# A streaming-encoder block on one core: a head's exponentials, normalisation, turning and values products on later steps, and the gates' functions 16 steps behind GpSimd's additions

## The chip, the core and the metric

The kernel runs on one core of a Trainium2 chip. The time is device time in microseconds (us). The engines are called as the profile calls them: PE is TensorE (its weight loads are PEld), DVE is VectorE, ACT is ScalarE, POOL is GpSimd, SP is SyncE, which here only issues DMAs.

## The reference

One layer over L = 512 tokens of width D = 2048, in float32. `proj = rmsnorm(x) @ w_in` is cut into the parts of two mixers and two merge gates. What the change touches, from the reference:

```python
logits = jnp.einsum('bqhd,bqkhd->bqkh', q_c, k_sel) * scale + bias      # 8 heads, head dim 128
logits = jnp.where(sel_ok[..., None], logits, -jnp.inf)                 # chunk-causal top-k keys
probs = jax.nn.softmax(logits, axis=2)
a_out = einsum('bqkh,bqkhd->bqhd', probs, v_sel) * jax.nn.silu(az)
b_out = retention_mixer(rq, rk, rv, ret_gn_gain) * jax.nn.silu(rz)
merged = jax.nn.sigmoid(ga) * (a_out @ w_a_out) + jax.nn.sigmoid(gb) * (b_out @ w_b_out)
r = x + merged @ w_o
return r + (p_i @ w_ple) * jax.nn.sigmoid(r @ w_ple_gate)               # and a last rmsnorm
```

The selection is kept as a mask over all keys, so that a head is a dense, causal attention over 512 tokens with a mask that is added to its bias.

## The kernel before

**Pairs.** A projection by two blocks of 128 weight columns (a pair) is done as seven Strassen-like products of 16 matmuls each (`gemm_pair`). Float32 is emulated with high and low parts: of each product's weights (128x1024) ScalarE casts the high part `wh` (L139) and VectorE subtracts it to get the low part `wl` (L144). Eight matmuls of 512 columns use `wh`, eight of 256 use `wl`; products 1, 4 and 6, counted from 0, begin with `wl`, the others with `wh`. Products 0 to 6 go to the PSUM banks `ps_v`, `ps_p`, `ps_q`, `ps_r`, `ps_p`, `ps_v`, `ps_p`. Behind a product ScalarE copies a bank (`pv` after product 0, `e` of L240 after products 1, 4 and 6), and VectorE subtracts or adds that copy to another bank (`e_t`, L244) after products 2, 5 and, twice, 6. Product 6 adds into the bank that `e` copies after product 4, so it starts behind that copy. A second function joins two `e_t` to the result; for a gate pair it adds on GpSimd (L960) where `adder=pool`, for a head's queries and keys on VectorE (L1041, `aq` and `ak`).

**Steps.** The program is issued in one order. Every two matmuls of a pair are one step, so that a product is 8 steps and a pair 56 (`PAIR_STEPS`); `later(n, f)` issues `f` n steps further on, and what is due at one step is issued in the order in which it was asked for. This decides where an instruction stands in the queue of its engine, and no engine passes over an instruction that waits. The weights' splits are issued two products ahead, at a product's first step, `wl` one step behind `wh`; there are three buffers each for `wh` and `wl`, and a split uses the one that the product before has given back. The raw weights are loaded by SP (7 buffers); some products need a second block added, by an accumulating DMA that GpSimd issues (L104) or by VectorE (L146).

**Order of the stages that the change touches.** Four pairs of `rz` (about 780 to 891 us): `b_out` (L1007) has ScalarE's Silu on the result `go`, GpSimd's multiplication with the retention output, and a DMA to `bd`, also issued by GpSimd. VectorE still does part of the top-k there (L723 to L726). Three pairs of `az` (891 to 951): Silu on ScalarE (L969) and a DMA to `zd` from ScalarE (L970). In both, `gate_pair` (L952) has `later(1, finish)` on L963: the function is issued one step behind GpSimd's second addition of that half. A pair's first half gets its second addition at step 48, the second half at 56.

Then eight pairs `u_qk`, one for each head (951 to 1145). A head's attention (`attention_head`, L1018) is issued during the next pair: four logits products (L1056, L808 to L810) with VectorE's addition and row maximum (L1058), the negated maximum `nm` (L1063) and four exponentials with their sums on ScalarE (`exps`, L1066), the reciprocal `ri` (L1070), the multiplication by it (`normalize`, three on ScalarE at L1076, one on VectorE at L1074), ten transpositions on TensorE (`turn`, L1085, `ps_pt`), their high parts `pth` on ScalarE (`high`, L1091 and L1094), the low parts `ptl` on VectorE (`low`, L1099), the values products (`outs`, L1111 and L1113, `ps_o`) already in the pair after that, the copy `oT` (L1117) and its store to `od`. The numbers in `steps` (L1122 to L1129) are the steps from the start of the pair that follows the head's own. Every three values products need a `ptl`: the first `outs` uses the one of 384 columns, the second the one of 256, the third the one of 512.

Last the fourth `az` pair (about 1145 to 1171), with the steps of head 7 and the loads and splits of `b_out` (`b_load`, `bk`, `bh`, `bl`), and the product with `w_b` (`project_b`), during which `a_load` fetches the heads' outputs and `zd`, multiplies them on GpSimd (L1152) and splits them for the product with `w_a`.

Of the kernel before, what the change touches and what calls it, by code (L numbers as in the profile page):

```python
# [34 lines left out]
def block_kernel(tc, xT, pT, posb, posq, w_in, w_v, w_k, w_a, w_b, w_o, w_ple, w_gate,  # L35
                 w_gt, w_pt, fgb, tab, xg, cst, dec, out, out_a, out_b):
    nc = tc.nc
    pe, dve, act, pool, sp = nc.tensor, nc.vector, nc.scalar, nc.gpsimd, nc.sync

    with contextlib.ExitStack() as ctx:  # L40
# [10 lines left out]
        def U(name, dt=F32):  # L51
            return up.tile([128, L], dt, name=name, tag="u")

        def B(name, dt=F32):
            return bp.tile([128, 1280], dt, name=name, tag="b")

        def P(name):
            return pp.tile([128, L], F32, name=name, tag="p")
# [4 lines left out]
        def tok(t):  # L63
            return slice(128 * t, 128 * t + 128)
# [96 lines left out]
        def later(n, f):  # L161
            if n <= 0:
                return f()
            tick[1] += 1
            heapq.heappush(soon, (tick[0] + n, tick[1], f))
# [49 lines left out]
        def alt(t, q):  # L215
            return t.rearrange("p (a s c) -> p a s c", s=2, c=64)[:, :, 0 if q == LO else 1, :]

        def fit(t, like):
            return t.rearrange("p (a c) -> p a c", c=like.shape[2]) if len(like.shape) == 3 else t
# [175 lines left out]
        for k in range(KT):  # L395
# [7 lines left out]
            elif k < 10:  # L403
                t = U("xk")
                sp.dma_start(t, xT[:, k, :])
                xs.append(t)
            elif k % 2 == 0:
                t = B("xk2")
# [390 lines left out]
        def split(src, name, lag=0):  # L799

            h = U(name + "h", F32R)
            l = U(name + "l", F32R)
            later(lag, lambda: act.activation(h, src, AF.Copy))
            later(lag and lag + 1, lambda: dve.tensor_sub(l, src, h.bitcast(F32)))
            return h, l
# [7 lines left out]
        yd, bd, od, zd = (dp.tile([NH, 128, L], F32, name=n) for n in ("yd", "bd", "od", "zd"))  # L813
# [138 lines left out]
        def gate_pair(ids, finish, wide=256, adder=None):  # L952
            t = B("go")
            outs = [t[:, 0:512], t[:, 512:1024]]
            have = [0, 0]

            def done(c0, c1, i, q):
                o = outs[i]
                to = alt(o, q)[:, 4 - wide // 64:, :]
                (adder or dve).tensor_add(to, fit(c0, to), fit(c1, to))  # L960
                have[i] += 1
                if have[i] == 2:
                    later(1, lambda: finish(i, o))  # L963

            gemm_pair(ids, Xh, done, wide=wide)

        def to(dst, func):
            def finish(i, o):
                act.activation(o, o, func)  # L969
                act.dma_start(dst[i], o)  # L970
            return finish
# [45 lines left out]
        aparts = []  # L1017
        def attention_head(h):  # L1018
            E = {}
# [30 lines left out]
            def logits(t):  # L1050
                ln = 128 * (t + 1)
                ps = P("ps_l")
                if t:
                    three(ps[:, :ln], E["aqs"], E["aks"], tok(t), slice(0, ln))
                else:
                    pe.matmul(ps[:, :ln], E["aq"][:, tok(t)], E["ak"][:, 0:ln], start=True, stop=True)  # L1056
                lg = E["bm"][:, TOFF[t]:TOFF[t] + ln]
                dve.tensor_tensor_reduce(out=lg, in0=ps[:, :ln], in1=lg, scale=1.0, scalar=-3e38,  # L1058
                                         op0=OP.add, op1=OP.max, accum_out=mx[:, t:t + 1])
# [20 lines left out]
            def turn(i):  # L1080
                ps = E["pt", i] = P("ps_pt")
                js = [(0, t) for t in range(4)] if i == 0 else [(1, 1), (1, 2), (1, 3), (3, 3)] if i == 1 \
                    else [(2, 2), (2, 3)]
                for n, (j, t) in enumerate(js):
                    pe.transpose(ps[:, tok(n)], E["bm"][:, TOFF[t] + 128 * j:TOFF[t] + 128 * j + 128], ident)  # L1085

            def high(i):
                if i == 0:
                    E["p"] = B("pth", F32R), B("ptl", F32R)
                n = (512, 384, 256)[i]  # L1090
                act.activation(E["p"][0][:, JOFF[i]:JOFF[i] + n], E["pt", i][:, 0:n], AF.Copy)  # L1091
                if i == 1:
                    E["p3"] = U("p3")
                    act.activation(E["p3"][:, 0:128], E["pt", i][:, 384:512], AF.Copy)  # L1094

            def low(i):
                n = (512, 384, 256)[i]
                c = slice(JOFF[i], JOFF[i] + n)
                dve.tensor_sub(E["p"][1][:, c], E["pt", i][:, 0:n], E["p"][0][:, c].bitcast(F32))  # L1099
# [4 lines left out]
            def outs(n):  # L1104
                if n == 0:
                    E["po"] = P("ps_o")
                po = E["po"]
                for i in range(3 * n, min(3 * n + 3, len(seq))):
                    a, b, j = seq[i]
                    if j == NT - 1:  # L1110
                        pe.matmul(po[:, 384:], E["v"][0][:, tok(3)].bitcast(F32), E["p3"][:, 0:128], start=False, stop=False)  # L1111
                    else:
                        pe.matmul(po[:, 128 * j:], E["v"][a][:, tok(j)], E["p"][b][:, JOFF[j]:JOFF[j] + L - 128 * j],  # L1113
                                  start=(i == 0), stop=(i == len(seq) - 1))
                if n == 3:
                    E["oT"] = U("oT")
                    act.activation(E["oT"], po, AF.Copy)  # L1117

            def store():
                sp.dma_start(od[h], E["oT"])  # L1120

            steps = [(-30, loads), (-8, mask), (30, values_load)]  # L1122
            steps += [(n, lambda t=t: logits(t)) for t, n in enumerate((20, 22, 24, 26))]
            steps += [(28, exps), (34, normalize)]
            steps += [(50, lambda i=i: turn(i)) for i in range(3)]
            steps += [(n, lambda i=i: high(i)) for i, n in enumerate((52, 52, 54))]
            steps += [(n, lambda i=i: low(i)) for i, n in enumerate((54, 54, 56))]
            steps += [(n, lambda i=i: outs(i)) for i, n in enumerate((65, 65, 69, 69))]
            steps += [(73 + STORE_LAG // 2, store)]  # L1129
            return done, steps  # L1130

        for n in range(Z_FIRST):
# [2 lines left out]
        for h in range(NH):  # L1135
            done, steps = attention_head(h)
            for n, f in steps:
                later(PAIR_STEPS + n, f)
            gemm_pair(u_qk[h], Xh, done)

        bparts = []

        def b_load(h):
            t = U("bk")
            sp.dma_start(t, bd[h])
            later(25, lambda: bparts.append(split(t, "b", 1)))

        def a_load(h):
            t, z = U("ak"), U("z")
            sp.dma_start(t, od[h])  # L1150
            sp.dma_start(z, zd[h])
            later(25, lambda: pool.tensor_mul(z, z, t))  # L1152
            later(29, lambda: aparts.append(split(z, "a", 1)))

        for n in range(Z_FIRST, NH // 2):
            if n == NH // 2 - 1:
                for h in range(NH):
                    later(4 + 3 * h, lambda h=h: b_load(h))
            gate_pair(u_az[n], to(zd[2 * n:2 * n + 2], AF.Silu), adder=pool)

        gates = collections.deque()
# [15 lines left out]
        for h in range(NH):  # L1177
            later(30 + 8 * h, lambda h=h: a_load(h))
# [6 lines left out]
        for m in PAIRED:  # L1185
            t = B("sm")
            s, o = t[:, 0:512], t[:, 512:1024]
# [96 lines left out]
        for m in range(MF):  # L1284
            i = u_p[m // 4][0]
# [3 lines left out]
            h, l = loaded[i]  # L1289
            ps = P("ps_pw")  # L1290
            for k in range(2):
                a, b = pparts[k]
# [5 lines left out]
            if m < Y_APART or m >= Y_APART + 2:  # L1298
                t = U("pw")
            else:  # L1300
                if m == Y_APART:
                    ypair[m // 2] = B("y2")
                t = ypair[m // 2][:, L * (m % 2):L * (m % 2) + L]
# [44 lines left out]
        for n in range(MF // 2):  # L1348
            t = B("go")
            outs = t[:, 0:512], t[:, 512:1024]  # L1350
# [108 lines left out]
        for o, c in zip(pw, HALF):  # L1459
            for j, (i, k) in enumerate(seq):  # L1460
                h, l = loaded[i]
                a, b = pparts[j][0][:, C3], pparts[j][1][:, C3]
# [23 lines left out]
        o = [U("yo") for _ in range(3)] + [s]  # L1486
# [32 lines left out]
Z_FIRST = 3  # L1519
ROUND_GAP = 11  # L1520
STORE_LAG = 16
# [97 lines left out]
```

## Time and profile before

| what | value |
|---|---|
| median of 3 timed runs | 1697.66 us (1697.63 to 1697.82) |
| profiled execution | 1698.91 us, of which the span shown is 1697.0 us |
| mean granted TensorE clock | 0.992 |
| busy PE, DVE, ACT, POOL | 98%, 81%, 55%, 18% of the span |
| instructions | 26283 |
| waits of PE between 780 and 1170 us | 27.0 us in 19 waits |
| waits of PE elsewhere | 1.8 us in the list of the largest |

All windows and times in the trace are us from the start of the span. In a row of the timeline stand the start, the duration, engine, line, operation, output and inputs with their shapes, and how many alike are joined ("x8"); a bracket gives how long the engine had been idle and what ended that. Matmuls overlap, so the distance between starts is what a group costs. In a row of the windows stand the busy times of PE, its weight loads, DVE, ACT and POOL, each with the number of instructions, then the granted clock, the DMA share and GB/s.

### The profile page before, as it was taken

The numbers are of one execution on the slowest core, as the hardware profiler recorded it, in microseconds if no ns is written. First come the engines' busy times: TensorE is split into PE (matmuls) and PEld (weight loads), VectorE is DVE, ScalarE is ACT, GpSimd is POOL, SyncE is SP. The second block draws the span as 40 slices with busy tenths as digits, with TensorE's granted clock in tenths as the row PEclk, the third lists the DMA queues.
The fourth block names the chain that finished last, engine by engine and source line by source line (L and its number), as shares of the span: only waits on it lengthen the run. The fifth ranks groups of instructions, "written<-read, shape, count | busy, mean of one in ns | idle before, by whom it ended". The sixth has DMA issues, their size and how long they took to land.

```text
span 1697.0 us, 26283 instructions
## 1 busy us (share of the span) xinstructions
PE 1660.6 (98%) x9600; PEld 1464.9 (86%) x9600; DVE 1369.1 (81%) x2189; ACT 939.4 (55%) x1437; POOL 305.3 (18%) x311
## 2 busy tenths in 40 slices
PE   9999999999999999999899999999999999999998
PEld 7999998888888888888778888888888888888897
DVE  8789887888889889889887676766548888899895
ACT  6557665555555555555444655565224455477673
POOL 3011111111111111112443111111200033411211
PEclk9999999999999999999999999999999999999999
DMA  8779888787887888877778987868866599999873
GB/s 292 263 236 254 210 206 203 198 215 184 224 215 202 212 212 212 212 209 219 215 187 217 246 193 213 213 177 272 285 237 196 159 253 284 265 323 238 217 241 125
DMA packets 141281, 379.02 MB, mean 223 GB/s; under 512 B 15328, under 2 KB 29792, under 8 KB 141152
## 3 DMA queue, kind: packets, MB, share of 16 engines
q1 hardware_dynamic: 105376, 261.20, 44.2%
q0 software_dynamic: 28144, 103.30, 33.9%
q10 hardware_dynamic: 7632, 12.85, 2.1%
q8 instruction: 76, 1.25, 0.3%
q14 instruction: 53, 0.43, 0.1%
HBM read 328.13 MB, written 49.15 MB: 222 GB/s over the span
## 4 chain that ended last, share of the span: by engine, by line
PE 83%; DVE 7%; ACT 4%; DMA 2%; issue 2%; POOL 1%; SPq 0%; POOLq 0%; ACTq 0%; DVEq 0%
PE ps_p L280 27%; PE ps_v L280 17%; PE ps_r L280 8%; PE ps_q L280 8%; DVE wl L144 3%; PE ps_vn L676 3%; PE ps_w L199 3%; PE ps_w L201 3%; PE ps_w L200 3%; ACT wh L139 1%; DMA xk<-xT 1%; ACT bm L1066 1%; PE ps_pt L1085 1%; PE ps_o L1113 1%; DVE bm L1058 1%
## 5 line engine op out<-in xcount | busy, mean ns | idle before, releaser
L144 DVE TENSOR_TENSOR wl<-wraw,wh 128x1024 fp32r<-128x1024 f32 (+2 forms) x501 | 613.0, 1227 | 182.2 <-ACT wh L139 174.3
L139 ACT ACTIVATE wh<-wraw 128x1024 fp32r<-128x1024 f32 (+2 forms) x500 | 514.8, 1039 | 314.2 <-DVE wraw L146 140.7
L104 POOL DMA_DIRECT2D wraw<-w_in x141 | 125.3, 921 | 804.6 <-DVE wl L144 343.8
L280 PE MATMUL ps_p<-hs,wh 128*128 128x512 f32 (+1 forms) x752 | 189.8, 394 | 0.0
L240 ACT ACTIVATE e<-ps_p 128x512 f32<-128x512 f32 (+1 forms) x183 | 108.0, 590 | 115.6 <-PE ps_p L280 110.2
L280 PEld LDWEIGHTS ps_p<-hs,wh 128*128 128x128 f32 x752 | 136.7, 192 | 24.6 <-issue 1.2
L280 PE MATMUL ps_p<-hs,wl 128*128 128x256 f32 (+1 forms) x752 | 111.4, 289 | 19.5 <-ACT e L240 15.4
L280 PEld LDWEIGHTS ps_p<-hs,wl 128*128 128x128 f32 x752 | 99.6, 195 | 22.6 <-ACT e L240 17.0
L280 PE MATMUL ps_r<-hs,wh 128*128 128x512 f32 (+1 forms) x376 | 98.8, 398 | 7.5 <-ACT wh L139 7.5
L280 PE MATMUL ps_p<-ha,wh 128*128 128x512 f32 (+1 forms) x376 | 95.4, 390 | 0.0
L280 PE MATMUL ps_v<-ha,wh 128*128 128x512 f32 (+1 forms) x376 | 92.9, 388 | 0.0
L280 PE MATMUL ps_v<-hs,wh 128*128 128x512 f32 (+1 forms) x376 | 92.2, 386 | 0.0
L280 PE MATMUL ps_q<-ha,wh 128*128 128x512 f32 (+1 forms) x376 | 92.1, 386 | 0.0
L280 PEld LDWEIGHTS ps_r<-hs,wh 128*128 128x128 f32 x376 | 68.0, 191 | 19.7 <-ACT wh L139 8.5
L280 PEld LDWEIGHTS ps_q<-ha,wh 128*128 128x128 f32 x376 | 70.1, 188 | 14.0 <-ACT wh L139 0.3
L280 PEld LDWEIGHTS ps_v<-hs,wh 128*128 128x128 f32 x376 | 70.2, 188 | 13.9
L280 PEld LDWEIGHTS ps_v<-ha,wh 128*128 128x128 f32 x376 | 69.6, 188 | 13.2
L280 PEld LDWEIGHTS ps_p<-ha,wh 128*128 128x128 f32 x376 | 67.2, 189 | 11.7 <-ACT wh L139 0.4
L146 DVE TENSOR_TENSOR wraw<-wraw 128x1024 f32<-128x1024 f32 x61 | 74.7, 1225 | 2.1
L676 PE MATMUL ps_vn<-wh,hh 128*128 128x296 f32 (+1 forms) x192 | 62.8, 332 | 0.4 <-DVE wh L137 0.3
L244 DVE TENSOR_TENSOR e_t<-ps_p,pv 128x512 f32<-128x512 f32 (+1 forms) x55 | 37.5, 681 | 30.7 <-ACT e L240 28.4
L676 PE MATMUL ps_vn<-wh,hl 128*128 128x296 f32 (+1 forms) x192 | 62.1, 329 | 0.0
(415 smaller groups left out, 3527.5 us busy)
## 6 DMA issues: line engine op xcount, KB each, us to landing
wraw<-w_in SPq DMA_DIRECT2D x192, 512.0 KB, 4.9
wraw<-w_in POOLq DMA_DIRECT2D x141, 512.0 KB, 7.8
wraw<-w_o SPq DMA_DIRECT2D x32, 512.0 KB, 6.7
wraw<-w_o POOLq DMA_DIRECT2D x24, 512.0 KB, 7.4
wraw<-w_gate SPq DMA_DIRECT2D x24, 512.0 KB, 5.7
wraw<-w_gate POOLq DMA_DIRECT2D x18, 512.0 KB, 7.1
wraw<-w_b SPq DMA_DIRECT2D x16, 512.0 KB, 5.2
wraw<-w_a SPq DMA_DIRECT2D x16, 512.0 KB, 4.3
```

Source lines behind the costliest of these rows:

```text
L104: pool.dma_start(out=raw_tiles[r], in_=src[:, k0:k0 + 8, :], accum_op=OP.add)
L139: act.activation(h, raw, AF.Copy)
L144: dve.tensor_sub(l, raw, h.bitcast(F32))
L146: dve.tensor_add(raw, raw, view(raw_tiles[plus], nk, cols))
L199: pe.matmul(o, h[:, k, w], a, start=(s == order[0]), stop=False)
L200: pe.matmul(o, h[:, k, w], b, start=False, stop=False)
L201: pe.matmul(o, l[:, k, w], a, start=False, stop=(s == order[-1]))
L240: act.activation(E[n], src, AF.Copy)
L244: f(t, x, y)
L280: pe.matmul(to, w[:, k], x, start=(n < 4 and part == parts[0] and k == order[0]), stop=(part == parts[1] and k == order[-1]), skip_group_c ...
L676: pe.matmul(pss[t], x[:, tok(t)], w[:, k], start=(s == 0 and n < NT * len(run) and x is a and w is h), stop=(s == KT - 1 and x is b))
L1058: dve.tensor_tensor_reduce(out=lg, in0=ps[:, :ln], in1=lg, scale=1.0, scalar=-3e38, op0=OP.add, op1=OP.max, accum_out=mx[:, t:t + 1])
```

## The change

Five edits. (1) In `gate_pair` the function of a pair whose additions are GpSimd's (four `rz`, four `az`) is issued 16 steps behind the second addition instead of one: at step 8 and 16 of the next pair. (2) In a head, `exps` goes from step 28 to 33, `normalize` from 34 to 44, the transpositions from 50 to 54, their high parts from 52, 52, 54 to 56, 56, 58, the low parts from 54, 54, 56 to 58, 58, 60, the values products from 65, 65, 69, 69 to 69, 69, 73, 73, and the store from 81 to 92. (3) For heads 0 to 5 the Silu gate `zd` is loaded within the head (step 48) and multiplied into `oT` on GpSimd (step 77), so that `od` holds the gated output. (4) `a_load` does this only for heads 6 and 7, and splits at 31 instead of 29 steps. (5) The loads of `b_out` start two steps earlier for the first heads and one step or more for the others, and their splits fall on steps 28, 30, 32 and then 39 + 2h instead of 29 + 3h.

```diff
--- before.py
+++ after.py
@@ -960,7 +960,7 @@
                 (adder or dve).tensor_add(to, fit(c0, to), fit(c1, to))
                 have[i] += 1
                 if have[i] == 2:
-                    later(1, lambda: finish(i, o))
+                    later(16 if adder else 1, lambda: finish(i, o))
 
             gemm_pair(ids, Xh, done, wide=wide)
 
@@ -1116,17 +1116,26 @@
                     E["oT"] = U("oT")
                     act.activation(E["oT"], po, AF.Copy)
 
+            def z_load():
+                if h < 2 * Z_FIRST:
+                    E["z"] = U("z")
+                    sp.dma_start(E["z"], zd[h])
+
+            def gate():
+                if h < 2 * Z_FIRST:
+                    pool.tensor_mul(E["oT"], E["z"], E["oT"])
+
             def store():
                 sp.dma_start(od[h], E["oT"])
 
             steps = [(-30, loads), (-8, mask), (30, values_load)]
             steps += [(n, lambda t=t: logits(t)) for t, n in enumerate((20, 22, 24, 26))]
-            steps += [(28, exps), (34, normalize)]
-            steps += [(50, lambda i=i: turn(i)) for i in range(3)]
-            steps += [(n, lambda i=i: high(i)) for i, n in enumerate((52, 52, 54))]
-            steps += [(n, lambda i=i: low(i)) for i, n in enumerate((54, 54, 56))]
-            steps += [(n, lambda i=i: outs(i)) for i, n in enumerate((65, 65, 69, 69))]
-            steps += [(73 + STORE_LAG // 2, store)]
+            steps += [(33, exps), (44, normalize)]
+            steps += [(54, lambda i=i: turn(i)) for i in range(3)]
+            steps += [(n, lambda i=i: high(i)) for i, n in enumerate((56, 56, 58))]
+            steps += [(n, lambda i=i: low(i)) for i, n in enumerate((58, 58, 60))]
+            steps += [(n, lambda i=i: outs(i)) for i, n in enumerate((69, 69, 73, 73))]
+            steps += [(48, z_load), (77, gate), (92, store)]
             return done, steps
 
         for n in range(Z_FIRST):
@@ -1143,19 +1152,21 @@
         def b_load(h):
             t = U("bk")
             sp.dma_start(t, bd[h])
-            later(25, lambda: bparts.append(split(t, "b", 1)))
+            later(26 + h if h < 3 else 40 - h, lambda: bparts.append(split(t, "b", 1)))
 
         def a_load(h):
-            t, z = U("ak"), U("z")
+            t = U("ak")
             sp.dma_start(t, od[h])
-            sp.dma_start(z, zd[h])
-            later(25, lambda: pool.tensor_mul(z, z, t))
-            later(29, lambda: aparts.append(split(z, "a", 1)))
+            if h >= 2 * Z_FIRST:
+                z = U("z")
+                sp.dma_start(z, zd[h])
+                later(26, lambda: pool.tensor_mul(t, z, t))
+            later(31, lambda: aparts.append(split(t, "a", 1)))
 
         for n in range(Z_FIRST, NH // 2):
             if n == NH // 2 - 1:
                 for h in range(NH):
-                    later(4 + 3 * h, lambda h=h: b_load(h))
+                    later(2 + h if h < 3 else 3 * h - 1, lambda h=h: b_load(h))
             gate_pair(u_az[n], to(zd[2 * n:2 * n + 2], AF.Silu), adder=pool)
 
         gates = collections.deque()
```

What this does to the queues, at three places. ScalarE in the second `rz` pair's end and the third's start; `go` is the gate result (L1007 its Silu), `wh` the weights' high parts, `e` and `pv` the copies of PSUM banks:

```order
 L139 ACTIVATE wh<-wraw 128x1024 x2
+L240 ACTIVATE e_9058<-ps_p 128x512
+L139 ACTIVATE wh<-wraw 128x1024
 L1007 ACTIVATE go<-go 128x512
-L240 ACTIVATE e_9061<-ps_p 128x512
+L240 ACTIVATE pv<-ps_v 128x512
 L139 ACTIVATE wh<-wraw 128x1024
 L1007 ACTIVATE go<-go 128x512
-L240 ACTIVATE pv<-ps_v 128x512
-L139 ACTIVATE wh<-wraw 128x1024
```

The Silu of the first half moved behind the copy `e` of product 6 and a `wh`, that of the second half behind `pv` and the next `wh`.

ScalarE in the middle of a head's steps, from the last exponentials on (`bm` holds the logits, `e` is the copy after product 4):

```order
 L1066 ACTIVATE bm,sums<-bm,nm 128x384
 L1066 ACTIVATE bm,sums<-bm,nm 128x512
+L240 ACTIVATE e_10670<-ps_p 128x512
 L139 ACTIVATE wh<-wraw 128x1024
 L1076 ACTIVATE bm<-bm,ri 128x128
 L1076 ACTIVATE bm<-bm,ri 128x256
 L1076 ACTIVATE bm<-bm,ri 128x384
-L240 ACTIVATE e_10673<-ps_p 128x512
-L139 ACTIVATE wh<-wraw 128x1024 x2
+L139 ACTIVATE wh<-wraw 128x1024
 L1047 ACTIVATE aq<-aq 128x512
```

The copy `e` now follows the exponentials directly; the `wh` that stood between them and the normalisation has moved ahead of the exponentials, and the normalisation follows the next `wh`.

VectorE around the end of a head's pair: `aql` and `akl` are the low parts of queries and keys, `ptl` those of the turned probabilities, `e_t` the sums after product 6. Before:

```order
L804 TENSOR_TENSOR aql<-aq,aqh 128x512
L1099 TENSOR_TENSOR ptl<-ps_pt,pth 128x512
L1099 TENSOR_TENSOR ptl<-ps_pt,pth 128x384
L1099 TENSOR_TENSOR ptl<-ps_pt,pth 128x256
L244 TENSOR_TENSOR e_t<-ps_p,pv 128x512
L1041 TENSOR_TENSOR ak<-e_t 128x4x64
L244 TENSOR_TENSOR e_t<-ps_r,e_11012 128x512
L1041 TENSOR_TENSOR ak<-e_t 128x4x64
L144 TENSOR_TENSOR wl<-wraw,wh 128x1024
L804 TENSOR_TENSOR akl<-ak,akh 128x512
```

The same place after the change:

```order
L804 TENSOR_TENSOR aql<-aq,aqh 128x512
L244 TENSOR_TENSOR e_t<-ps_p,pv 128x512
L1041 TENSOR_TENSOR ak<-e_t 128x4x64
L244 TENSOR_TENSOR e_t<-ps_r,e_11016 128x512
L1041 TENSOR_TENSOR ak<-e_t 128x4x64
L144 TENSOR_TENSOR wl<-wraw,wh 128x1024
L1099 TENSOR_TENSOR ptl<-ps_pt,pth 128x512
L1099 TENSOR_TENSOR ptl<-ps_pt,pth 128x384
L804 TENSOR_TENSOR akl<-ak,akh 128x512
L1099 TENSOR_TENSOR ptl<-ps_pt,pth 128x256
```

The three `ptl` moved behind both sums, the two `ak` and a `wl`, and `akl` stands between the second and the third.

## The prediction

> **What bounds the kernel now.** I read the page's busy table first, then TensorE's waits over the span, then windows cut where the wait list points, and the timeline of one such place.
>
> ```profile
> PE 1660.6 (98%) x9600; PEld 1464.9 (86%) x9600; DVE 1369.1 (81%) x2189; ACT 939.4 (55%) x1437; POOL 305.3 (18%) x311
> ```
>
> TensorE (PE) is the bound: a change can only win what TensorE idles, or what its clock loses. Its waits, with the total in us, the count and the longest:
>
> ```profile
> PE ps_p L280 <- ACT e L240: 15.4, 8, 2.9
> PE ps_r L280 <- ACT wh L139: 7.5, 5, 2.0
> PE ps_p L280 <- DVE wl L144: 3.5, 5, 1.3
> PE ps_p L280 <- ACT wh L139: 0.6, 1, 0.6
> ```
>
> These four make 27.0 us. The first is one wait in each attention head; the other three lie in the gate pairs. The windows (window, us, then busy time of PE, PEld, DVE, ACT and POOL, then granted clock, DMA share and GB/s) show how much longer the pairs take than they need:
>
> ```profile
> 798.70:911.96 113.26, 101.66 (x552) 87.51 (x551) 92.97 (x159) 51.11 (x66) 52.32 (x51) 0.97 0.78 205
> 798.70:823.15 24.45, 21.12 (x119) 18.17 (x118) 19.99 (x43) 10.53 (x14) 11.22 (x12) 1.00 0.76 205
> 931.45:950.95 19.50, 19.50 (x115) 17.22 (x114) 12.68 (x14) 10.41 (x14) 6.04 (x6) 1.00 0.95 244
> 972.20:1164.00 191.80, 179.30 (x1009) 159.41 (x1008) 131.25 (x225) 114.50 (x213) 25.28 (x28) 0.96 0.78 211
> 1000.10:1026.30 26.20, 24.45 (x144) 21.69 (x144) 18.66 (x33) 16.04 (x31) 3.51 (x4) 1.00 0.80 218
> ```
>
> The first row is five gate pairs and the third is one that nothing disturbs: 113.26 - 5 x 19.50 = 15.8 us. The fourth row is seven head pairs and the fifth is one of them at full clock, with its wait still in it. Their mean clocks of 0.97 and 0.96 are .03 x 113.26 + .04 x 191.8 = 11.1 us lost. Where the clock goes is seen at a gate stall of 2.03 us, beside a stretch of a head that runs at full clock:
>
> ```profile
> 878.35 3.18 PE L280 MATMUL ps_r<-hs,wh 128*128 128x512 f32 x8 [2.03 <-ACT wh L139]
> 881.33 1.64 PE L280 MATMUL ps_r<-hs,wl 128*128 128x256 f32 x8
> 880.00:881.00 1.00, 1.00 (x4) 0.76 (x3) 0.97 (x4) 0.00 (x0) 0.00 (x0) 0.50 1.09 217
> 876.24 0.63 ACT L1007 ACTIVATE go<-go 128x512 f32<-128x512 f32 x1 [3.35 <-POOL go L960]
> 994.34 1.12 PE L280 MATMUL ps_p<-hs,wl 128*128 128x256 f32 x8
> 995.30 2.00 PE L280 MATMUL ps_p<-hs,wh 128*128 128x512 f32 x8
> 997.14 1.98 PE L280 MATMUL ps_v<-ha,wh 128*128 128x512 f32 x8
> 998.96 1.11 PE L280 MATMUL ps_v<-ha,wl 128*128 128x256 f32 x8
> ```
>
> After this stall the granted clock was 0.50 in the microsecond from 880. Eight `wh` matmuls took 878.35 to 881.33, 2.98 us, where 995.30 to 997.14, 1.84 us, is normal; with the eight `wl` behind them (1.64 against 1.11) that is some 1.6 us a time, so that 11.1 us are seven such stretches, two in the gate pairs and five in the heads. The ACT row shows the culprit: ScalarE stood at L1007 for GpSimd's addition, with the weight cast `wh` queued behind it.
>
> **Gate functions 16 steps later.** A step is two matmuls, so 16 steps are some 5.6 us of a 19.50 us pair (56 steps). The first half's function now comes behind the pair's last `e` and a `wh`, the second's behind `pv` and a `wh`; GpSimd's sums were 3.35 us late for the old place and are about 2 us early for the new one. So `wh` comes in time, and with it the 7.5 and 0.6 us, the two clock losses (3.4 us) and most of the 3.5 us of `wl`. The moved function brings its neighbours: GpSimd's multiplication and its DMA (rz pairs) or ScalarE's DMA (az) move past one weight addition each (L104); nobody waits for these stores before the attention stage. What is late next is VectorE: 19.99 us of work in the first pair where 19.50 are to be had, and still top-k work in the next three. From nothing more than .5 us up to the whole 3.5 us of `wl` can stay; I leave 1.5, plus .9 for the extra matmuls in the first two pairs: 15.8 - 2.4 = **13.4 us**.
>
> **Attention steps later: what goes.** One head, engine by engine:
>
> ```profile
> 995.33 0.40 ACT L1066 ACTIVATE bm<-bm,nm 128x128 f32<-128x128 f32 x1 [2.90 <-DVE nm L1063]
> 997.53 1.04 ACT L139 ACTIVATE wh<-wraw 128x1024 fp32r<-128x1024 f32 x1
> 1000.01 1.30 ACT L1076 ACTIVATE bm<-bm,ri 128x128 f32<-128x128 f32 x3 [1.44 <-DVE ri L1070]
> 1001.22 0.57 ACT L240 ACTIVATE e<-ps_p 128x512 f32<-128x512 f32 x1
> 1001.70 1.99 ACT L139 ACTIVATE wh<-wraw 128x1024 fp32r<-128x1024 f32 x2
> 1001.85 0.75 PE L280 MATMUL ps_p<-hs,wl 128*128 128x256 f32 x4 [1.78 <-ACT e L240]
> 1005.85 1.98 PE L280 MATMUL ps_v<-hs,wh 128*128 128x512 f32 x8
> ```
>
> The copy `e` of product 4 was ready to go at 997.34 (product 4 ends at 997.14, plus .2), and stood behind the exponentials, `wh` and the normalisation until 1001.22. The last product could have begun at 998.96 + .96 = 999.92 (eight `wl` matmuls are .96 from 994.34 to 995.30), so TensorE lost 1.93 us. A head without it: 26.20 - 1.93 = 24.3 us; 191.8 - 7 x 24.3 = 21.7 us (seven waits and the half clock after five of them). The eighth wait, the longest of the list with 2.9 us, lies behind these windows and adds 3.0: **24.7 us** to be had.
>
> **What comes new.** After the change `wh` goes ahead of the exponentials and `e` directly behind them. That `wh` takes the buffer that product 3 gives back at 994.34, so it runs 994.54 to 995.5, in the old wait for `nm`; exponentials 995.52 to 997.72 (2.20 as before), `e` then, done by 998.3: the old wait is gone with 1.6 us to spare. The rest of the chain, starts only, each by the distance of the rows above and of those below (`e` to `wh` .48, `wh` to `wl` 1.07, `wl` to `ri` 1.15, `ri` to the normalisation .26, from there to the next 1.21): `wh` 998.20, `wl` 999.27, `ri` 1000.42, normalisation 1000.68 to 1001.98, `wh` 1001.89, `wl` 1002.96. The transpositions stand 12 matmuls into product 6, at 999.92 + 1.9 = 1001.8, and need the normalised rows at 1002.2: .4 us. Then VectorE, before the change:
>
> ```profile
> 998.60 1.23 DVE L144 TENSOR_TENSOR wl<-wraw,wh 128x1024 fp32r<-128x1024 f32 x1 [3.31 <-ACT wh L139]
> 999.75 0.17 DVE L1070 RECIPROCAL ri<-sums 128x4 f32<-128x4 f32 x1
> 1006.43 0.69 DVE L804 TENSOR_TENSOR aql<-aq,aqh 128x512 fp32r<-128x512 f32 x1 [0.23 <-ACT aqh L803]
> 1007.04 1.48 DVE L1099 TENSOR_TENSOR ptl<-ps_pt,pth 128x512 fp32r<-128x512 f32 x3
> 1008.44 0.68 DVE L244 TENSOR_TENSOR e_t<-ps_p,pv 128x512 f32<-128x512 f32 x1
> 1009.50 0.68 DVE L244 TENSOR_TENSOR e_t<-ps_r,e 128x512 f32<-128x512 f32 x1
> 1008.62 0.40 PE L280 MATMUL ps_p<-ha,wl 128*128 128x256 f32 x2
> 1008.86 0.57 PE L1113 MATMUL ps_o<-pth,av 128*128 128x512 f32 x2
> 1009.27 0.35 PE L1113 MATMUL ps_o<-ptl,av 128*128 128x384 f32 x1
> 1009.75 0.28 PE L1113 MATMUL ps_o<-ptl,av 128*128 128x256 f32 x1
> ```
>
> The low parts `ptl` (512, 384, 256 wide) were made before the two sums `e_t`; now they stand behind both sums, their `ak`, and one more `wl`. From `wl` at 1002.96: `aql` 1004.11 (+1.15), `e_t` 1004.72 (+.61), second `e_t` 1005.78 (+1.06), `wl` 1006.84, `ptl` 512 at 1007.99, `ptl` 384 at 1008.59 (the three take 1007.04 to 1008.44, by width .60, .46 and .34) and there for TensorE about 1009.1; `akl` now comes between, so `ptl` 256 is there about 1010.1. On TensorE product 6 takes 3.80 us with its transpositions, ends at 1003.72 + .4 = 1004.1, and the values products, moved by four steps, begin 26 matmuls on (1005.85 to 1008.62 = 2.77, plus .96 and .46): 1008.3. The third of them needs `ptl` 384 at .41 later, 1008.7: it waits .4; the sixth needs `ptl` 256 .48 after that and waits another .45. Sum: .4 + .4 + .45 = **1.3 us of new waits a head** in six heads.
>
> The first head has a table load that was covered by the wait for `nm`:
>
> ```profile
> 964.61 1.28 ACT L1066 ACT_TABLE_LOAD   x1
> ```
>
> It now comes behind the `wh` of 994.54's kind and delays that head's whole chain: 1.3 + 1.3 = 2.6 us. The last head runs in a gate pair without `aq` and `ak` on VectorE; I take .4. New waits: 6 x 1.3 + 2.6 + .4 = 10.8 us; attention gains 24.7 - 10.8 = **13.9 us**. The bounds of the 1.3 are 0 (a chain .9 us shorter and transpositions in time) and the old 1.78 with its half clock.
>
> **The gate multiplications moved into the heads.**
>
> ```profile
> L1152 POOL TENSOR_TENSOR z<-z,ak x8: 1287/1292/1304, 1194.0 to 1233.2; 128x512 f32<-128x512 f32 x8
> 916.97 2.41 POOL L960 TENSOR_TENSOR go<-e_t 128x256 f32<-128x256 f32 x2 [1.66 <-DVE e_t L244]
> 917.39 1.39 DVE L144 TENSOR_TENSOR wl<-wraw,wh 128x1024 fp32r<-128x1024 f32 x1
> ```
>
> Six multiplications of 1.29 us go to GpSimd, which is busy 3.51 us of a head's 26.2; the only row behind them is a weight addition that is due a product later. Each head also loads .26 MB of `z`: 218 GB/s x 26.2 us = 5.71 MB become 5.97 in 25.6 us, 233 GB/s, under the 244 that the window from 931.45 carried. The store waits for the multiplication on the SP queue, with weight loads behind it, 15 steps after the multiplication is issued: 5 us against 1.29. The b loads and splits, and the a splits two steps later, fall where TensorE waits for none of them. All nothing; what the neighbourhood costs is in the second and third row: a `wl` beside GpSimd took 1.39 us where 1.23 is usual. "SBUF — State Buffer" of the Trainium skill, section "SBUF: two separate sides", says that VectorE and GpSimd hold a shared port pair exclusively and the loser blocks for the whole instruction; the trace shows .16 us, not 1.29. By the page the time would be about 1677.
>
> **The sum.** The profiled execution took 1698.91 us (span 1697.0), 1.25 above the median of the timed runs. 1698.91 - 13.4 - 13.9 = 1671.6, so about **1670** for the median. The chain can be off by .5 us in seven heads and the gate rest by 1.5: 1665 to 1675.
>
> **Rivals.** (A) No new wait decides: the `ptl` come in time, and only the table load costs: 1697.7 - 13.4 - 24.7 + 1.3 = 1661. For it: my chain rests on steps of a tenth each; against it: `ptl` moved back by four VectorE rows and `outs` by four steps only. (B) The new waits bring the half clock in each head, 7 x 1.6: 1681. For it: five of the seven old waits did; against: it is split in three pieces of .45, and the gate pair from 798.70 has 24.45 - 21.12 = 3.3 us of waits at a clock of 1.00. (C) VectorE bounds the gate pairs: all 3.5 us of `wl` waits stay, and the sums come late for the new place too, +6: 1676. (D) The clock drops are not due to the waits and stay: 7 x 1.6 more, 1681. "TensorE: Matmul & The Clock Gate" of the Trainium skill, "Part 1: The HAM clock gate", has half rate only after an idle window of about 3.4 us, by which waits of 1.78 could not cause it; the 0.50 right behind the 2.03 us stall speaks for the waits. (E) The port lock above, on the head's chain: six heads x 1.1 (1.29 less .2 that exponentials now have on `nm`): 1677. (F) Slower: the values products become the wait. Per head it must cost more than (38 + 3.4)/8 = 5.2 us: with the half clock's 1.6, 3.6 us of waiting, so `ptl` 256 2.3 us later than I reckon, at 1012.4. That takes VectorE holding two more `wl` ahead of `ptl`, by a late weight.
>
> **How the numbers follow.** What can be told from no change here is 0.2%, 3.4 us. Chances: forecast .57, A .15, B .09, C .06, D .04, E .03, F .06, of which a third lands within 0.2%. So faster .94, same .02, slower .04. The range 1660 to 1682 takes in A, C, E and half of B and D, and leaves out F, the rest of these and the far end of A.
>
> **What would show it.** Right: no TensorE wait on `e` L240 in the heads, none on `wh` in the gate pairs; new rows "ps_o waits for ptl L1099" of some .9 us a head and short ones of `ps_pt` for `bm`; head pairs near 25.6 us with the clock at 1.00; gate pairs of 19.5 to 20.5. Wrong: waits on `e` that remain, `ps_o` waits over 1.8 us or a clock under 1.00 in the heads, gate pairs over 21 us, or SP's weight loads standing behind a store.

## The result and the profile after

| | before | after |
|---|---|---|
| median of the timed runs, us | 1697.64 (1697.16 to 1697.82, 4 runs) | 1682.8 (1681.6 to 1685.05, 4 runs) |
| profiled execution, us | 1698.91 (span 1697.0) | 1682.58 (span 1680.6) |
| mean granted clock | 0.992 | 0.997 |

The ratio is 0.9915, with a 95% interval from 0.9897 to 0.9932: 14.8 us faster, where 27.6 us were forecast. The measured time lies 0.8 us above the range. The changed kernel's four runs spread over 3.5 us, the four of the kernel before over 0.7; on the chips of the experiments, though, the kernel before spread over 4.8 to 11.5 us.

TensorE's waits after the change, in the view shown before:

```profile
PE ps_o L1113 <- DVE ptl L1099: 11.2, 14, 1.5
PE ps_p L280 <- DVE wl L144: 4.3, 7, 0.7
PE ps_q L280 <- DVE wl L144: 1.0, 1, 1.0
PE ps_p L280 <- ACT wh L139: 0.6, 1, 0.6
PE ps_pt L1085 <- ACT bm L1076: 0.3, 2, 0.2
```

The waits on `e` and `ps_r` on `wh` (22.9 us) are gone. New are fourteen waits on `ptl`, two in each of seven heads; and the waits on `wl`, 3.5 us before, have grown to 5.3. Together 17.4 us stand where 27.0 stood.

To see where the 16.3 us between the two profiled executions lie, both spans are cut at the same instruction, the start of a pair's first product. By these starts, and not by the times given with the stages above, TensorE does the four `rz` pairs of the kernel before from 775.38 to 867.82 us, the three `az` pairs to 934.09 and the eight `u_qk` pairs to 1143.51. Before, five gate pairs (`rz` and `az`) and then six head pairs:

```profile
798.96:914.60 115.64, 104.03 (x566) 89.62 (x564) 94.64 (x161) 51.34 (x67) 54.15 (x54) 0.97 0.79 207
979.60:1143.51 163.91, 153.22 (x865) 136.15 (x864) 112.30 (x193) 97.22 (x181) 21.07 (x25) 0.96 0.77 203
```

The same after, and below them two single heads of the second row:

```profile
798.28:904.31 106.03, 100.12 (x566) 86.88 (x564) 103.41 (x161) 52.99 (x67) 56.01 (x53) 1.00 0.85 221
966.27:1127.74 161.47, 151.92 (x865) 131.53 (x864) 117.42 (x193) 96.95 (x181) 31.89 (x30) 0.98 0.84 216
966.27:992.74 26.47, 24.80 (x145) 21.50 (x144) 19.67 (x33) 16.09 (x31) 5.34 (x5) 1.00 0.87 226
992.74:1020.76 28.02, 26.36 (x146) 22.77 (x145) 20.03 (x33) 16.53 (x32) 4.80 (x5) 0.94 0.84 213
```

The gate pairs give 9.6 us, the six head pairs 2.4, the first head's pair and the last pair behind them another 3.6 (3.0 and 0.5, by the starts of the pairs), and 0.7 lie ahead of all that the change touches. A head at full clock takes 26.25 or 26.47 us, not the 25.6 forecast, and no less than the 26.24 or 26.25 before. What these six gained is mostly the clock, and not all of it: four of them showed 0.94 before, and two still do.

VectorE's busy time is the other thing to see. In the five gate pairs it rose from 94.64 to 103.41 us with the same 161 instructions. Something made them longer.

### The profile page after: what moved, and what is told of

It is laid out like the page before. It is cut to its first block, busy times and chain, and to the rows that moved or that the text cites. A ratio compares the mean times of both kernels' runs of the same rounds, so it can differ in the third digit from the quotient of the medians.

```text
span 1680.6 us, 26284 instructions
## 1 busy us (share of the span) xinstructions
PE 1653.6 (98%) x9600; PEld 1455.6 (87%) x9600; DVE 1378.4 (82%) x2189; ACT 939.0 (56%) x1437; POOL 311.6 (19%) x311
## 4 chain that ended last, share of the span: by engine, by line
PE 82%; DVE 9%; ACT 4%; DMA 3%; issue 2%; POOL 1%; SPq 0%; POOLq 0%; ACTq 0%; DVEq 0%
PE ps_p L280 25%; PE ps_v L280 16%; PE ps_q L280 9%; PE ps_r L280 9%; DVE wl L144 4%; PE ps_vn L676 4%; PE ps_w L199 3%; PE ps_w L200 3%; PE ps_w L201 3%; DVE e_t L244 1%; DVE isc L724 1%; ACT wh L139 1%; DMA xk<-xT 1%; DVE m L723 1%; ACT bm L1066 1%
## 5 line engine op out<-in xcount | busy, mean ns | idle before, releaser
L280 PE MATMUL ps_p<-hs,wl 128*128 128x256 f32 (+1 forms) x752 | 106.3, 283 | 4.9 <-DVE wl L144 4.3
L280 PEld LDWEIGHTS ps_v<-hs,wh 128*128 128x128 f32 x376 | 70.2, 188 | 13.9
L146 DVE TENSOR_TENSOR wraw<-wraw 128x1024 f32<-128x1024 f32 x61 | 79.7, 1307 | 2.1
```

Of the source, the lines that this page charges most:

```text
L146: dve.tensor_add(raw, raw, view(raw_tiles[plus], nk, cols))
L280: pe.matmul(to, w[:, k], x, start=(n < 4 and part == parts[0] and k == order[0]), stop=(part == parts[1] and k == order[-1]), skip_group_c ...
```

## The experiments

The prediction left two things to explain: why the heads' new waits cost about 2 us each and not 1.3, and why the `wl` waits in the gate pairs grew. The runs were made on several chips; each ratio is to the kernel before on the same chip.

**The parts alone.** The first kernel is the one before with the gate edit:

```diff
-                    later(1, lambda: finish(i, o))
+                    later(16 if adder else 1, lambda: finish(i, o))
```

> The kernel before with the first edit alone (gate functions 16 steps later). If the profile after is read rightly, the gate pairs give 9.6 us (five pairs 115.6 to 106.0 us) and the heads stay as they were, with eight waits on e and half clocks: 1697.6 - 9.6 = 1688. By the prediction's sum, 13.4 us: 1684. The wl waits behind GpSimd's multiplications (wl of 2.2 to 5.0 us) should be there as in the profile after.

Measured: 1687.61 us against 1698.49 on the same chip, ratio 0.9933 (0.9918 to 0.9948).

The second is the changed kernel with that edit undone:

```diff
-                    later(16 if adder else 1, lambda: finish(i, o))
+                    later(1, lambda: finish(i, o))
```

> The changed kernel with the first edit undone (functions one step behind the additions). If the profile after is read rightly, the heads give some 6 us, nearly all of it from the clock: 1697.6 - 6 = 1691, with waits for ptl of 1.5 + 0.2 us a head; by the prediction's sum 13.9 us: 1684. If the two parts disturb one another, the two gains don't add up to the 14.8 us of the whole.

Measured: 1693.55 us against 1698.49, ratio 0.9972 (0.9960 to 0.9984). So the parts give 10.9 and 4.9 us, which together are about the whole; they hardly disturb one another. The heads fall far short of the 13.9 us forecast. For the gate edit the interval, 8.8 to 13.9 us, leaves open whether it does; the five pairs of its profile take 106.1 us, as in the whole change.

**The heads: what makes `ptl` late.** The profile after, VectorE first, then ScalarE and TensorE at the same place:

```profile
991.80 1.23 DVE L144 TENSOR_TENSOR wl<-wraw,wh 128x1024 fp32r<-128x1024 f32 x1 [0.80 <-ACT wh L139]
992.99 0.69 DVE L804 TENSOR_TENSOR aql<-aq,aqh 128x512 fp32r<-128x512 f32 x1
994.51 0.69 DVE L244 TENSOR_TENSOR e_t<-ps_p,pv 128x512 f32<-128x512 f32 x1 [0.82 <-ACT e L240]
997.77 1.15 DVE L1099 TENSOR_TENSOR ptl<-ps_pt,pth 128x512 fp32r<-128x512 f32 x2
...
992.86 0.96 ACT L1091 ACTIVATE pth<-ps_pt 128x512 fp32r<-128x512 f32 x2
993.71 0.28 ACT L1094 ACTIVATE p<-ps_pt 128x128 f32<-128x128 f32 x1
993.87 0.61 ACT L240 ACTIVATE e<-ps_p 128x512 f32<-128x512 f32 x1
...
988.78 1.12 PE L280 MATMUL ps_p<-hs,wl 128*128 128x256 f32 x8
992.74 1.99 PE L280 MATMUL ps_v<-hs,wh 128*128 128x512 f32 x8
996.95 0.57 PE L1113 MATMUL ps_o<-pth,av 128*128 128x512 f32 x2
998.98 0.44 PE L1113 MATMUL ps_o<-ptl,av 128*128 128x384 f32 x1 [1.46 <-DVE ptl L1099]
999.91 0.39 PE L1113 MATMUL ps_o<-ptl,av 128*128 128x256 f32 x1 [0.20 <-DVE ptl L1099]
```

The prediction set product 6 at 999.92; here it starts at 988.78, so its times are to be read 11.14 lower. Its `wl` of 1002.96 becomes 991.82: measured 991.80. Its `aql` of 1004.11 becomes 992.97: measured 992.99. Its `e_t` of 1004.72 becomes 993.58: measured 994.51. The chain is right to two hundredths up to there, and then .93 us are lost in one link: `e_t` of `ps_p` and `pv` waits for ScalarE's `e`, the copy of the same bank, which stands behind three instructions on `ps_pt` (two `pth` and one `p`). It doesn't read that copy, and no run shows why it waits; but in the profiles of before and after no such `e_t` of these stages starts earlier than .03 us behind the end of `e`. Nothing after that is later than reckoned. The third kernel takes `pth` out of the way of `e`:

```diff
-            steps += [(n, lambda i=i: high(i)) for i, n in enumerate((56, 56, 58))]
-            steps += [(n, lambda i=i: low(i)) for i, n in enumerate((58, 58, 60))]
+            steps += [(n, lambda i=i: high(i)) for i, n in enumerate((57, 57, 59))]
+            steps += [(n, lambda i=i: low(i)) for i, n in enumerate((59, 59, 61))]
```

> The changed kernel with pth at steps 57, 57, 59 and ptl at 59, 59, 61, so that on ScalarE the copy e of product 6 stands ahead of the pth instead of behind them; VectorE's order stays as it is. Theory: the sum e_t on VectorE waits for this e (0.82 us in the profile after), and this is what makes ptl late; then e_t and all behind it come 0.8 us earlier, the wait for the 384-wide ptl falls from 1.46 to about 0.65 us in seven heads, and the half clock goes: 1682.8 - 6 - 3 = 1674 to 1677. Rival: VectorE's own queue (the two sums and wl ahead of ptl) sets it, or pth themselves are late: waits as before, 1682.

Measured: 1674.38 us (1673.62 to 1675.79), ratio 0.9858 (0.9842 to 0.9875). In its trace the sum follows `aql` at once, and the waits shrink by that much:

```profile
991.65 0.69 DVE L804 TENSOR_TENSOR aql<-aq,aqh 128x512 fp32r<-128x512 f32 x1
992.26 0.68 DVE L244 TENSOR_TENSOR e_t<-ps_p,pv 128x512 f32<-128x512 f32 x1
995.52 1.15 DVE L1099 TENSOR_TENSOR ptl<-ps_pt,pth 128x512 fp32r<-128x512 f32 x2
...
996.72 0.44 PE L1113 MATMUL ps_o<-ptl,av 128*128 128x384 f32 x1 [0.55 <-DVE ptl L1099]
997.65 0.39 PE L1113 MATMUL ps_o<-ptl,av 128*128 128x256 f32 x1 [0.20 <-DVE ptl L1099]
```

`e_t` starts .61 behind `aql`, as the prediction had it, VectorE's order is unchanged, and the wait for the 384-wide `ptl` is 0.55 where it was 1.46. So the failed link is the wait for `e`, not VectorE's own queue.

The fourth kernel leaves the chain as the change made it and moves what waits for it:

```diff
-            steps += [(n, lambda i=i: outs(i)) for i, n in enumerate((69, 69, 73, 73))]
-            steps += [(48, z_load), (77, gate), (92, store)]
+            steps += [(n, lambda i=i: outs(i)) for i, n in enumerate((73, 73, 77, 77))]
+            steps += [(48, z_load), (81, gate), (92, store)]
```

> The changed kernel with the values products four steps later again (73, 73, 77, 77) and the multiplication by the gate at 81. Theory: TensorE reaches the ptl 1.4 us too early and nothing else of a head is late, so the wait of 1.46 us goes to 0.1 and no clock drop is left: 7 x 1.4 + 3 = 13 us, 1670. Rival: the heads are held by something that a ptl wait covers (a weight, another wait that shows when this is gone): less than half of it, 1676 or more.

Measured: 1665.62 us (1665.27 to 1665.90), ratio 0.9805 (0.9790 to 0.9819). One head, then five in a row, from its windows:

```profile
990.72:1015.07 24.35, 24.35 (x146) 21.59 (x145) 18.85 (x33) 16.09 (x31) 4.82 (x5) 1.00 0.92 246
990.72:1112.66 121.94, 121.94 (x721) 108.00 (x720) 94.37 (x161) 80.45 (x151) 24.13 (x25) 1.00 0.90 237
```

TensorE is busy throughout, at full clock: 24.39 us a head. This is the undisturbed head that the prediction had worked out as 24.3, and it is had without touching the chain. Nothing else was waiting behind the `ptl` wait. The time is 4 us lower than expected, mostly because a head's two waits of 1.46 and 0.20 had cost it 1.9 us and not 1.4. The four runs lie within 0.6 us.

**The gate pairs: who makes `wl` long.** In the profile after, one `wl` on VectorE, GpSimd beside it, and TensorE:

```profile
865.20 5.01 DVE L144 TENSOR_TENSOR wl<-wraw,wh 128x1024 fp32r<-128x1024 f32 x1
...
865.26 1.71 POOL L960 TENSOR_TENSOR go<-e_t 128x256 f32<-128x256 f32 x2
867.25 1.87 POOL L1008 TENSOR_TENSOR go<-go,y 128x512 f32<-128x512 f32 x1
870.15 1.31 POOL L1008 TENSOR_TENSOR go<-go,y 128x512 f32<-128x512 f32 x1
...
870.26 1.22 PE L280 MATMUL ps_q<-ha,wl 128*128 128x256 f32 x8 [1.01 <-DVE wl L144]
```

A `wl` of 1.22 us took 5.01, over two additions and a multiplication of GpSimd; TensorE waited for it. The next three kernels all start from the one with the values products at 73 and 77 (1665.62 us), since its heads add no scatter. They ran on another chip than that one, and the intervals of some of the ratios overlap; so their five gate pairs are compared as well. The fifth leaves the multiplication out:

```diff
-                pool.tensor_mul(o, o, y[i])
```

> The changed kernel with the values products four steps later (as in the run before it) and without GpSimd's multiplication of the rz gates with the retention output (L1008), so the gate alone is stored: this part of the computation is left out. Theory: the wl that run beside this multiplication are held up by it (2.2, 3.0, 3.0 and 5.0 us instead of 1.22), and of the 5.9 us of wl waits in the gate pairs those early in a pair (0.74, 0.68, 1.01, 0.59 us) come from that: they go, the five pairs fall from 106.1 to about 102.5 us, the time from 1665.6 to 1662. Rival: VectorE is simply full there (top-k): the wl are as long, or the waits stay, 1665.

Measured: 1658.80 us (1657.98 to 1659.58), ratio 0.9769 (0.9751 to 0.9786). The five gate pairs and the `wl` at that same place:

```profile
797.85:896.66 98.81, 98.25 (x566) 86.62 (x564) 96.20 (x161) 53.56 (x67) 45.39 (x45) 1.00 0.90 228
...
859.95 2.88 DVE L144 TENSOR_TENSOR wl<-wraw,wh 128x1024 fp32r<-128x1024 f32 x1
```

The five pairs take 98.8 us where the kernel that it starts from takes 106.1, and all waits on `wl` are gone, not just those early in a pair that the theory gave to GpSimd. VectorE still has all its top-k work, 96.20 us in 98.81, and TensorE doesn't wait for it. A VectorE that is 97% busy was enough as long as only the additions held it up (the `wl` of 2.88 us); it was the delay from the multiplication, passed along a full queue through the rest of the pair, that made the later waits as well.

The sixth does that multiplication on VectorE:

```diff
-                pool.tensor_mul(o, o, y[i])
-                pool.dma_start(out=bd[2 * n + i], in_=o)
+                later(4, lambda: dve.tensor_mul(o, o, y[i]))
+                later(4, lambda: pool.dma_start(out=bd[2 * n + i], in_=o))
```

> The same kernel (values products four steps later) with that multiplication on VectorE, four steps later than it was on GpSimd, its DMA still on GpSimd. If the hold-up beside GpSimd costs more than the work itself (1.4 us a pair on VectorE against some 2 to 4 us of longer wl), 1663 to 1665; if VectorE's load is what counts, it has 1.4 us more in each of four pairs that are full already: 1668 or more.

Measured: 1662.42 us (1662.19 to 1662.70), ratio 0.9790 (0.9773 to 0.9807). Doing 1.4 us a pair itself is cheaper for VectorE than being held up: its busy time in the five pairs falls from 103.5 to 100.9 us, and the pairs take 102.9. But it is not enough. With no multiplication left on GpSimd, TensorE still waits for `wl`:

```profile
PE ps_p L280 <- DVE wl L144: 2.5, 4, 0.9
```

The seventh leaves GpSimd alone and gives VectorE room:

```diff
-BG_RATES = (3, 3, 4, 10, 8, 9)
+BG_RATES = (3, 3, 4, 10, 8, 11)
```

> The same kernel (values products four steps later) with the top-k rounds on VectorE issued every 11 steps instead of every 9 in this stage, so that they reach into the next pairs, where VectorE works 12 of 19.5 us. Theory: the waits of about 0.65 us late in each pair and part of those early in it are top-k work ahead of a wl in a full queue; they shrink by a half or more: 1662 to 1664. Rival: they come from the order at single places or from GpSimd alone: 1665.6 as before.

Measured: 1660.68 us (1660.20 to 1662.92), ratio 0.9783 (0.9762 to 0.9805). A `wl` of 5.00 us is still in its trace (at 860.20), the five pairs take 100.0 us, and of 6.0 us of waits 1.9 are left. So neither condition does it all: a `wl` held up by GpSimd becomes a wait above all where VectorE is too full to catch up before TensorE wants the next, and a fuller VectorE makes some waits without the multiplication. The theory had the two causes apart; they act on one queue.

The last kernel has the edits of the sixth and the seventh together:

> The changed kernel with the values products four steps later, the top-k rounds every 11 steps and the multiplication of the rz gates on VectorE: both remedies together. If the remaining 1.6 us of wl waits with rate 11 come from the wl that GpSimd holds up (3 to 5 us), they go as well and the time falls from 1660.7 to about 1659, where the kernel without the multiplication was (1658.8); if VectorE's added 1.4 us a pair fill the room that the slower rounds gave, it stays at 1660.7 or rises towards 1662.4.

Measured: 1657.06 us (1656.35 to 1657.41), ratio 0.9750 (0.9725 to 0.9775), against 1699.44 on that chip. The gate pairs and four heads, with TensorE busy from end to end:

```profile
797.18:895.08 97.90, 97.90 (x566) 86.52 (x564) 96.05 (x157) 53.55 (x67) 41.07 (x43) 1.00 0.90 238
1006.18:1103.76 97.58, 97.58 (x577) 86.42 (x576) 75.50 (x129) 64.37 (x121) 19.30 (x20) 1.00 0.90 235
```

It beats both kernels, the changed one by some 26 us. A few numbers and one moved multiplication bring more than the change itself did.

## Why the prediction missed

**The old waits.** Right. All waits on `e` and on `ps_r` went, and a head without waits is 24.39 us (24.3 forecast).

**The new waits in the heads.** The mechanism, the place and the tile were right, the size was not: 1.3 us a head were forecast, 1.9 to 2.1 came in seven pairs (26.25 and 26.47 less 24.39). The step that failed is "`aql` 1004.11 (+1.15), `e_t` 1004.72 (+.61)". It took the distance from the old rows, in which `e_t` waited for nothing, and asked only whether VectorE was free. Before the change three `ptl` stood between `aql` and `e_t` and covered the copy `e`; taking them away uncovered it. The row for it lay in the trace of before:

```profile
1007.57 0.62 ACT L240 ACTIVATE e<-ps_p 128x512 f32<-128x512 f32 x1
```

It ends at 1008.19, a quarter of a microsecond ahead of the sum; without the three `ptl`, VectorE would have been free for the sum at 1007.04, long before that end. The term should have gone over ScalarE's queue, `aq`, `aqh`, `pth`, `e`, as it went over VectorE's. Two other terms did not come, and that hid a part of the miss. The transpositions start at 990.67, as reckoned (1001.8 less 11.14), and wait for nothing; the waits on `bm` are 0.3 us in all heads together, not .4 in each. And the first head's table load, priced at 1.3 us, hardly shows: TensorE waits .18 us in that head's pair, and 1.47 for its 384-wide `ptl`, as for the others'.

**The half clock.** The forecast had none in the heads, rival B one in each. Two of six came, 1.6 to 1.8 us longer than their neighbours at full clock. With .93 less in the wait (the third kernel) none is seen in the heads, so that this too hangs on the failed step.

**The gate pairs.** 9.6 us in the profile, 10.9 in the run of that edit alone, against 13.4. `wh` came as reckoned but for one wait of 0.6, and the clock was 1.00; the step that failed is "I leave 1.5" of waits on `wl`: 5.9 us stayed (0.6 of them on `wh`). It named VectorE's top-k load, and the run without the multiplication shows that load alone to cost nothing. What the sum missed is that the moved multiplications now stand beside a `wl`; the prediction asked of them only who waits for their stores.

That only 3.8 us are missing is in part luck. The prediction's window of five gate pairs ended at 911.96, and the fifth pair ends at 914.60; cut there, and with the 19.50 us of an undisturbed pair (the window shown for it lies nearly all in the first `u_qk` pair, but the third `az` pair takes 19.49 too), the five had 18.1 us to give (115.64 - 5 x 19.50), not 15.8, and after the change 8.5 are left where 2.4 were forecast. Nor do the clock and the waits on `wl` simply add. The pair with the stall at 878.35 is in the first row; below it is TensorE in the same pair of the kernel with the heads' edits alone:

```profile
867.82:891.21 23.39, 21.36 (x113) 18.55 (x112) 18.29 (x31) 10.19 (x13) 11.14 (x12) 0.93 0.71 181
...
877.29 2.12 PE L280 MATMUL ps_r<-hs,wh 128*128 128x512 f32 x8 [2.05 <-ACT wh L139]
880.81 1.22 PE L280 MATMUL ps_p<-hs,wl 128*128 128x256 f32 x8 [0.46 <-DVE wl L144]
887.27 1.19 PE L280 MATMUL ps_p<-hs,wl 128*128 128x256 f32 x8 [0.64 <-DVE wl L144]
```

There the stall left the clock at 1.00, and the pair (866.75 to 890.14) still takes 23.39 us: waits on `wl`, of which the pair of the first row has none, stand where the half clock stood.

**The multiplications moved into the heads.** Nothing was forecast, and nothing they cost: the head of 24.39 us contains one. But the reason given was wrong. Here is one of them, and VectorE beside it, in the profile after:

```profile
977.36 1.83 POOL L1126 TENSOR_TENSOR oT<-z,oT 128x512 f32<-128x512 f32 x1 [6.74 <-ACT oT L1117]
...
978.08 2.20 DVE L146 TENSOR_TENSOR wraw<-wraw 128x1024 f32<-128x1024 f32 x1
```

VectorE's addition took 2.20 us instead of 1.23: GpSimd ended at 979.19, and nearly a full addition (1.09 us) lies behind that. It is hidden there, in a head where VectorE works 18.9 of 24.4 us. The prediction had priced such a meeting at .16 us, from a `wl` of 1.39 beside GpSimd's additions (L960). That was the wrong pair of rows: in it GpSimd came second and paid, its second addition (917.67) taking 1.71 us where the first took 0.73. The right rows were in the profile of before, where a multiplication met a `wl`:

```profile
1211.81 1.29 POOL L1152 TENSOR_TENSOR z<-z,ak 128x512 f32<-128x512 f32 x1 [4.49 <-DMA z<-zd]
1211.85 2.33 DVE L144 TENSOR_TENSOR wl<-wraw,wh 128x1024 fp32r<-128x1024 f32 x1 [0.17 <-ACT wh L139]
```

GpSimd ends at 1213.10, and `wl` at 1214.18, with nearly all of its own 1.22 us behind that. This is what the Trainium skill, "SBUF — State Buffer", section "SBUF: two separate sides", says: the two share a port pair under an exclusive lock that is held for the whole instruction, and the other one blocks. The prediction weighed that rule, gave it .03 and looked for it in the heads. The trace agrees with the page, in that one blocks for the other's whole instruction; which of the two it is doesn't follow from the starts in the records (last section). It decided in the gate pairs.

**The range.** Each rival was priced against the forecast by itself. A part of B (two half clocks) and a loss in the gate pairs like C's, though smaller and not for C's reason, came together with a head chain some .6 us too short: about 3.4 + 3.8 + 7 x .6 = 11.4 us, where the profiled execution lies 11.0 above the 1671.6 of the sum. No rival had two of them at once.

## What to carry to other kernels

When instructions are moved, look at what now comes earlier, and follow everything that it waits for through the queue of the engine that makes it; a distance read from old rows holds only as long as the same things cover it. For a resource that two engines share, find the rows in which the engine you care about is the one held up, and ask of every moved operation what it now runs beside. And when a consumer waits for a long chain, moving the consumer by a few steps can be worth more than shortening the chain: four steps gave 17 us here.

## What the runs showed of the hardware

One and the same wait brings the half clock or doesn't. In the kernel with the gate edit alone, the waits on `e` are 1.78 or 1.79 us in seven heads, and the distances between them are 26.2 us after some and 27.8 after others; in the one with the heads' edits alone, waits of 2.05 and 1.87 us in the gate pairs left the clock at 1.00. In the heads it never came without a wait: the kernels of 24.39 us a head show 1.00 throughout, which speaks against rival D. "TensorE: Matmul & The Clock Gate" of the Trainium skill, "Part 1: The HAM clock gate", names a window of about 3.4 us that runs freely; waits of 1.5 to 2.0 us are shorter than that and did bring the half clock, so its figure for the idle time isn't borne out here. That the phase of the window decides would fit the draws, but no run here shows it.

The hold-up by GpSimd doesn't follow the starts in the records: the `wl` of 5.01 us starts at 865.20, .06 us ahead of the addition, and yet ends at 870.21, 1.1 us behind the end of the multiplication that came later still (869.12). So one `wl` can lose to several GpSimd instructions in a row, 3.8 us here. Another in the same profile starts .37 us ahead of a multiplication and ends 1.10 behind it:

```profile
826.51 3.05 DVE L144 TENSOR_TENSOR wl<-wraw,wh 128x1024 fp32r<-128x1024 f32 x1
826.88 1.58 POOL L1008 TENSOR_TENSOR go<-go,y 128x512 f32<-128x512 f32 x1
```
